# Scores of both components in one two-bank PSUM tile: a two-layer hybrid encoder on one core

## The chip, the core and the metric

The kernel runs on one core of a Trainium2 chip. The core has a matmul engine (TensorE, PE in the profile; its weight loads are listed apart as PEld), a vector engine (DVE), a scalar engine for activations (ACT), a general engine (POOL) and queues that start transfers (SP). PE writes its products into PSUM. Each engine works through its own list of instructions in order and waits on semaphores for the others. The metric is the device time of one execution in microseconds (us); less is better. PSUM is used here as eight banks of 128 partitions by 512 float32 numbers.

## What is computed

A trunk of two encoder layers over 512 tokens of width 1024, in float32:

```python
for l in range(DEPTH):                          # DEPTH = 2
    h = rmsnorm(x, g_attn[l])
    proj = jnp.einsum('bsd,dc->bsc', h, w_in[l])
    qa, ka, va, qb, kb, vb = jnp.split(proj, offs, axis=-1)
    # group A: 8 query heads, 2 kv heads of 64, blocks of 128, keys of +-1 block, a sink per head
    ya = windowed_gqa_sink(qa, ka, va, sink[l])         # after QK-norm and rotary
    # group B: 4 heads, each with two components of 64; softmax of each; values of 128
    #   w = p[:, :, 0] - lam * p[:, :, 1]
    yb = rmsnorm(diff_attention(qb, kb, vb, lam), subln[l]) * (1.0 - lambda_init)
    y = jnp.concatenate([ya, yb], axis=-1)
    x = x + jnp.einsum('bsm,md->bsd', y, w_out[l])
    h = rmsnorm(x, g_ffn[l])
    gate, val = jnp.split(jnp.einsum('bsd,df->bsf', h, w_up[l]), 2, axis=-1)
    gate = centred_dwconv(gate, conv_w[l], conv_b[l])   # width 3 over the tokens
    x = x + jnp.einsum('bsf,fd->bsd', jax.nn.silu(gate) * val, w_down[l])
```

d_ff is 2816, 22 blocks of 128.

## The kernel before

**Products.** Every float32 operand is split into a high and a low part, and a product is three matmuls (high by high, low by high, high by low; the helper `mm3`, L193 to L196). Activations lie transposed: features on partitions, the 512 tokens along the row. Weights come as units of 512 KB or less; ACT makes the high part (L181), DVE or POOL the low one (L182).

**A layer.** The first norm is folded into the input projection (`project`), which runs over nine chunks of 256 columns by four token tiles: akv (keys and values of group A), aq0 and aq1 (its queries), and bv, bq, bk of the two halves of group B. Then attention, the output projection, a second norm, and the feed-forward part (FFN) in two parts of 12 and 10 blocks: for each block gate and value (`up`), the convolution and the gate on DVE, ACT and POOL, and after each part the down projection `dn` into eight output tiles, which DVE adds to the residual (L716).

**Group A**, for each of 2 head pairs `ip` and 4 query blocks `qb`: `a_scores` makes scores for 2 query heads i by 2 kv heads g. The product for g reads the 64 rows of its own half of the array (rows 0 to 63 or 64 to 127), so two neighbours with different g use different halves. DVE adds the mask and takes the maximum (L416), ACT the exponential (L434), DVE normalises (L441). `a_values` transposes the weights on PE, one bank per key block (`pt_a`, L457), splits them (L246, L247) and multiplies by the values (`pv_a`).

**Group B**, for each half, query block and head: `b_scores` makes the scores of both components c, again on the two halves of the array (L502); a maximum for each (L505), an exponential for each (L509), and their difference. `b_values` transposes (`wt_b`, L529) and multiplies by the values (`yb`).

**Banks.** `mm`: two banks, for the projections and the output projection while attention runs. `at`: four single banks, for akv, part of aq, all scores and the transposed weights. `acc`: one for sums over key blocks. `tq`: one, for the transposes of queries, keys and results. In the FFN, for `dn` and for the last pass of the output projection (`out_last(1)`), `wide` (L109) rotates at, at, mm. A tile of a tag waits until the oldest tile of that tag has been read for the last time.

**Order.** `weave` (L665) writes two tracks into each other by cost: attention, and a chain of bv, bq, bk of the two halves and of the output projection. The framework's scheduler then puts each engine's instructions in order by its own times, with the waits that tiles and tags demand.

## Time and profile before

| | |
|---|---|
| median of 3 runs | 1309.32 us (1308.12 to 1310.32) |
| span of the profiled execution, first to last instruction | 1302.4 us |
| time of that execution outside the span | not shown; the median is 6.9 us above its span |
| mean granted TensorE clock | 0.991 |
| busy: PE, PEld, DVE, ACT, POOL | 1270.6, 1056.6, 772.9, 557.5, 385.4 us |
| data moved by the transfers | 102.96 MB, 79 GB/s on the mean |

The profile is of one execution. A row of a group names the line, the engine, the operation, output and inputs with their shapes, the count, then busy us in total, mean ns of one, and the engine's idle time just before with what ended it. A row of the timeline has start and duration in us; matmuls are pipelined, so the distance of two starts, not the duration, is what one costs. A row of windows has the stretch, its length, and for each engine the busy us and the number of instructions, then the granted clock as a share of full speed, the transfers' share and GB/s. The attention of layer 0 lies at about 30 to 290 us, its FFN behind that up to about 650; layer 1 follows in the same way.

### The profile page before, as it was taken

The numbers are of one execution on the slowest core, as the hardware profiler recorded it, in microseconds if no ns is written. First come the engines' busy times: TensorE is split into PE (matmuls) and PEld (weight loads), VectorE is DVE, ScalarE is ACT, GpSimd is POOL, SyncE is SP. The second block draws the span as 40 slices with busy tenths as digits, with TensorE's granted clock in tenths as the row PEclk, the third lists the DMA queues.
The fourth block names the chain that finished last, engine by engine and source line by source line (L and its number), as shares of the span: only waits on it lengthen the run. The fifth ranks groups of instructions, "written<-read, shape, count | busy, mean of one in ns | idle before, by whom it ended". The sixth has DMA issues, their size and how long they took to land. (4 is left out here: it accounts for less than half of the span.)

```text
span 1302.4 us, 17571 instructions
## 1 busy us (share of the span) xinstructions
PE 1270.6 (98%) x6744; PEld 1056.6 (81%) x6744; DVE 772.9 (59%) x1425; ACT 557.5 (43%) x1027; POOL 385.4 (30%) x446
## 2 busy tenths in 40 slices
PE   6999899999999999999999999999899999999998
PEld 6988788687888888888899878877788888888887
DVE  7678787767655324554466786767765543355532
ACT  4566555435433223333455656544443332233321
POOL 6847376114211000110156654741411110011100
PEclk8999999999999999999999999999999999999999
DMA  5211112113332233332331211111133322433232
GB/s 181 91 33 49 58 33 65 33 33 97 98 97 85 85 106 97 98 97 79 100 98 66 65 33 33 56 59 33 33 113 97 97 81 94 117 98 98 79 106 90
DMA packets 32628, 102.96 MB, mean 79 GB/s; under 512 B 3616, under 2 KB 4000, under 8 KB 32544
## 3 DMA queue, kind: packets, MB, share of 16 engines
q1 hardware_dynamic: 32544, 101.84, 25.6%
q8 instruction: 53, 0.87, 0.3%
q14 instruction: 31, 0.25, 0.1%
HBM read 99.73 MB, written 2.10 MB: 78 GB/s over the span
## 5 line engine op out<-in xcount | busy, mean ns | idle before, releaser
L181 ACT CAST wh<-wr 128x1024 fp32r<-128x1024 f32 (+3 forms) x210 | 197.7, 944 | 400.1 <-PE up L195 192.0
L195 PE MATMUL up<-nf_l,wh 128*128 128x512 f32 x704 | 275.3, 391 | 2.3 <-DVE nf_l L213 1.9
L196 PE MATMUL up<-nf_h,wl 128*128 128x512 f32 x704 | 274.5, 390 | 1.2 <-DVE wl L182 0.9
L194 PE MATMUL up<-nf_h,wh 128*128 128x512 f32 x704 | 272.9, 390 | 0.0
L182 DVE TENSOR_TENSOR wl<-wr,wh 128x1024 fp32r<-128x1024 f32 (+3 forms) x174 | 193.3, 1114 | 112.2 <-ACT wh L181 111.8
L702 POOL TENSOR_TENSOR cv<-cv,rb 128x512 f32<-128x512 f32 x44 | 57.8, 1316 | 521.5 <-ACT cv L701 521.5
L195 PEld LDWEIGHTS up<-nf_l,wh 128*128 128x128 f32 x704 | 132.1, 188 | 33.6 <-DVE nf_l L213 6.6
L196 PEld LDWEIGHTS up<-nf_h,wl 128*128 128x128 f32 x704 | 132.1, 188 | 29.7 <-DVE wl L182 2.9
L194 PEld LDWEIGHTS up<-nf_h,wh 128*128 128x128 f32 x704 | 132.2, 188 | 27.6
L195 PE MATMUL dn<-act,wh 128*128 128x512 f32 x352 | 138.5, 394 | 0.0
L196 PE MATMUL dn<-act,wl 128*128 128x512 f32 x352 | 138.4, 394 | 0.0
L194 PE MATMUL dn<-act,wh 128*128 128x512 f32 x352 | 137.9, 393 | 0.0
L182 POOL TENSOR_TENSOR wl<-wr,wh 128x1024 fp32r<-128x1024 f32 x36 | 87.1, 2421 | 89.4 <-ACT wh L181 89.4
L695 DVE TENSOR_TENSOR gp<-up,rb 128x512 f32<-128x512 f32 x44 | 30.3, 693 | 103.4 <-PE up L196 101.8
L703 DVE TENSOR_TENSOR cv<-cv,up 128x512 f32<-128x512 f32 x44 | 30.2, 687 | 82.6 <-POOL cv L702 73.0
L194 PEld LDWEIGHTS dn<-act,wh 128*128 128x128 f32 x352 | 66.0, 188 | 16.0
L195 PEld LDWEIGHTS dn<-act,wh 128*128 128x128 f32 x352 | 66.0, 187 | 15.7
L196 PEld LDWEIGHTS dn<-act,wl 128*128 128x128 f32 x352 | 66.0, 188 | 15.4
L716 DVE TENSOR_TENSOR x<-x,dn 128x512 f32<-128x512 f32 x32 | 22.0, 689 | 78.4 <-PE dn L196 78.4
L509 ACT ACTIVATE e_b<-sc_b,mx_b,rqb 128x512 f32<-128x512 f32 x64 | 49.2, 774 | 38.6 <-DVE mx_b L506 38.6
L701 ACT ACTIVATE cv<-cv 128x512 f32<-128x512 f32 x44 | 27.8, 632 | 76.4 <-DVE cv L700 76.3
L505 DVE TENSOR_REDUCE mx_b<-sc_b 128x1 f32<-128x512 f32 x64 | 42.0, 681 | 0.2
(211 smaller groups left out, 2713.7 us busy)
## 6 DMA issues: line engine op xcount, KB each, us to landing
wr<-w_up SPq DMA_DIRECT2D x88, 512.0 KB, 3.6
wr<-w_in SPq DMA_DIRECT2D x36, 512.0 KB, 3.7
wr<-w_down SPq DMA_DIRECT2D x32, 384.0 KB, 3.1
wr<-w_down SPq DMA_DIRECT2D x32, 320.0 KB, 2.9
wr<-w_out SPq DMA_DIRECT2D x16, 512.0 KB, 3.6
x<-xT SPq DMA_DIRECT2D x8, 256.0 KB, 5.3
outT<-x SPq DMA_DIRECT2D x8, 256.0 KB, 2.0
rows<-row_par SPq DMA_DIRECT2D x2, 260.0 KB, 5.0
```

Of the source, the lines that this page charges most:

```text
L181: nc.scalar.copy(hi[:, o], raw[:, o])
L182: eng.tensor_tensor(out=lo[:, o], in0=raw[:, o], in1=hi[:, o], op=ALU.subtract)
L194: nc.tensor.matmul(acc, lhsT=a[0], rhs=b[0], start=start, stop=False)
L195: nc.tensor.matmul(acc, lhsT=a[0], rhs=b[1], start=False, stop=False)
L196: nc.tensor.matmul(acc, lhsT=a[1], rhs=b[0], start=False, stop=stop)
L505: nc.vector.tensor_reduce(out=mx[:, c:c + 1], in_=sc[c], axis=AX, op=ALU.max)
L509: nc.scalar.activation(e[c], sc[c], AF.Exp, bias=mx[:, c:c + 1], scale=rq[:, c:c + 1], accum_out=lsum[:, 2 * j + c:2 * j + c + 1])
L695: nc.vector.tensor_tensor(out=g[:, 1:S + 1], in0=acc[0], in1=rb, op=ALU.mult)
L701: nc.scalar.activation(cv, cv, AF.Silu)
L702: nc.gpsimd.tensor_tensor(out=cv, in0=cv, in1=rb, op=ALU.mult)
L703: nc.vector.tensor_tensor(out=cv, in0=cv, in1=acc[1], op=ALU.mult)
L716: nc.vector.tensor_tensor(out=x_sb[d], in0=x_sb[d], in1=acc, op=ALU.add)
```

## The change

The four single banks `at` become two tiles of two banks each (`at2`). `both` hands out the two banks of such a tile; `halves` hands them out one after the other; `wide2` hands out pairs, every third one of two `mm` banks. The scores of one query head for both kv heads share a tile, and so do both components of a step of group B, whose two maxima become one reduction of a [128, 2, 512] tile to [128, 2]. Gate and value of a block share a pair. The akv projection, the four middle tiles of aq, `out_last(1)` and `dn` take halves in turn. In `a_values` the transposes go to the first bank of an `at2` tile for key block 0 (the second stays unused), to `tq` for key block 1 and to `mm` for key block 2; in `b_values` `wt` goes to the first bank of an `at2` tile, or as before to `mm` for the second head of the second half. No arithmetic changes.

```diff
@@ -95,8 +95,8 @@
     def mm(name):
         return ps.tile([P, S], F32, tag="mm", bufs=2, name=name)
 
-    def at(name):
-        return ps.tile([P, S], F32, tag="at", bufs=4, name=name)
+    def at2(name):
+        return ps.tile([P, 2, S], F32, tag="at", bufs=2, name=name)
 
     def accum(name):
         return ps.tile([P, S], F32, tag="acc", bufs=1, name=name)
...
@@ -106,9 +106,25 @@
 
     cyc = {"i": 0}
 
-    def wide(name):
+    def wide2(name):
         cyc["i"] += 1
-        return (mm, at, at)[cyc["i"] % 3](name)
+        if cyc["i"] % 3 == 0:
+            return mm(f"{name}a"), mm(f"{name}b")
+        t = at2(name)
+        return t[:, 0], t[:, 1]
+    def halves(pick):
+        have = []
+        def alloc(name):
+            if not have:
+                have.extend(pick(name))
+            return have.pop(0)
+        return alloc
+    def both(name):
+        t = at2(name)
+        return t[:, 0], t[:, 1]
 
     def run(gen):
         for _ in gen:
...
@@ -375,7 +391,7 @@
             split_out(va[0][:, t * P:(t + 1) * P], va[1][:, t * P:(t + 1) * P], raw[:, P:])
             qk_out(raw[:, :P], t, P, tabs[1], ka, "ka", None)
 
-        run(project("akv", akv_done, at))
+        run(project("akv", akv_done, halves(both)))
         rqa = sb.tile([P, NT, 4, 2], F32, tag="rqa", bufs=1, name=f"rqa{l}")
         rqb = sb.tile([P, NT, 4, 2], F32, tag="rqb", bufs=1, name=f"rqb{l}")
         qa = [(pair(f"qah{l}_{i}"), pair(f"qal{l}_{i}")) for i in range(2)]
...
@@ -385,7 +401,8 @@
                 bank, t, CW, tabs[0], qa[i], f"qa{i}", rqa[:, t, 2 * i:2 * i + 2, :].rearrange("p a b -> p (a b)")), alloc)
 
         qk = {}
-        banks = iter((mm, mm, at, at, at, at, mm, mm))
+        pairs_at = halves(both)
+        banks = iter((mm, mm, pairs_at, pairs_at, pairs_at, pairs_at, mm, mm))
         run(proj_a(0, lambda name: next(banks)(name)))
         run(proj_a(1, lambda name: next(banks)(name)))
 
...
@@ -405,7 +422,7 @@
             mx = small(f"mx_{nm}", 4)
             so = []
             for i in range(2):
-                sc = [at(f"sc_{nm}_{i}_{g}") for g in range(2)]
+                sc = both(f"sc_{nm}_{i}")
                 for j, (u, v) in enumerate(((0, 0), (0, 1), (1, 0))):
                     for g in range(2):
                         rs = slice(g * HD, (g + 1) * HD)
...
@@ -450,7 +467,7 @@
             pv = accum(f"pv_{nm}")
             pb = []
             for b in range(nkb):
-                tr = at(f"pt_{nm}_{b}")
+                tr = mm(f"pt_{nm}_{b}") if b == 2 else both(f"pt_{nm}_{b}")[0] if b == 0 else tq(f"pt_{nm}_{b}")
                 for g in range(2):
                     for i in range(2):
                         o = (2 * g + i) * P
...
@@ -495,14 +512,14 @@
             rq = rqb[:, qb, h, :]
             q, k = qk[half]
             e = []
-            sc = [at(f"sc_{nm}_{c}") for c in range(2)]
+            sc2 = at2(f"sc_{nm}")
+            sc = (sc2[:, 0], sc2[:, 1])
             for i, (u, v) in enumerate(((0, 0), (0, 1), (1, 0))):
                 for c in range(2):
                     rs = slice(c * HD, (c + 1) * HD)
                     nc.tensor.matmul(sc[c], lhsT=q[u][rs, j, qb * P:(qb + 1) * P], rhs=k[v][rs, j, :],
                                      start=i == 0, stop=i == 2)
-            for c in range(2):
-                nc.vector.tensor_reduce(out=mx[:, c:c + 1], in_=sc[c], axis=AX, op=ALU.max)
+            nc.vector.tensor_reduce(out=mx, in_=sc2, axis=AX, op=ALU.max)
             nc.vector.scalar_tensor_tensor(out=mx, in0=mx, scalar=-1.0, in1=rq, op0=ALU.mult, op1=ALU.mult)
             for c in range(2):
                 e.append(tmp(f"e_{nm}_{c}"))
...
@@ -524,7 +541,7 @@
                 b_st[half, qb, "acc"] = accum(f"yb{l}_{half}_{qb}")
             yb = b_st[half, qb, "acc"]
             w = b_st.pop((half, qb, j))
-            tr = (mm if half and j else at)(f"wt_{nm}")
+            tr = mm(f"wt_{nm}") if half and j else both(f"wt_{nm}")[0]
             for b in range(NT):
                 nc.tensor.transpose(tr[:, b * P:(b + 1) * P], w[:, b * P:(b + 1) * P], ident)
             wh, wl = prob(f"wth_{nm}"), prob(f"wtl_{nm}")
...
@@ -664,7 +681,7 @@
 
         weave((attend(), ATT),
               (chain(proj_b(0), proj_b(1), out_pass(0, mm), out_pass(1, mm), out_tail()), 98.6))
-        run(out_last(1, w_last, wide))
+        run(out_last(1, w_last, halves(wide2)))
         norm.square(NK - 2)
         norm.square(NK - 1)
         r_tok2 = norm.rms()
...
@@ -675,20 +692,18 @@
         rb = tmp(f"rb{l}")
         nc.scalar.copy(rb, rps)
 
         h = norm
         if l + 1 < depth:
             norm = Norm(l + 1, 0, f"na{l + 1}")
         for pi, (f0, f1) in enumerate(FF_PARTS):
             act = []
             for f in range(f0, f1):
-                acc = []
+                acc = wide2(f"up{l}_{f}")
                 for j in range(2):
                     w = next_unit()
-                    a = wide(f"up{l}_{f}_{j}")
                     for k in range(NK):
-                        mm3(a, (w[0][:, k, :], w[1][:, k, :]), (h.hi[k], h.lo[k]), k == 0, k == NK - 1)
-                    acc.append(a)
+                        mm3(acc[j], (w[0][:, k, :], w[1][:, k, :]), (h.hi[k], h.lo[k]), k == 0, k == NK - 1)
                 g = tmp(f"gp{l}_{f}", S + 2)
                 nc.gpsimd.memset(g[:, 0:1], 0.0)
                 nc.gpsimd.memset(g[:, S + 1:S + 2], 0.0)
...
@@ -705,6 +720,7 @@
                 split_out(a[:, 0], a[:, 1], cv)
                 act.append((a[:, 0], a[:, 1]))
             last = pi == len(FF_PARTS) - 1
+            wide = halves(wide2)
             for d in range(NK):
                 acc = wide(f"dn{l}_{pi}_{d}")
                 nk = f1 - f0
```

What this does to the order of PE's instructions is shown at three places. Lines of the changed kernel lie some 16 to 18 further down; a number behind a tile's name counts buffers, `[waits X]` names the engine whose signal the instruction waits for, x2 is a count of alike neighbours.

**Scores of group B** (layer 0, second half; `sc_b0_2_1_1` is head 2, query block 1, component 1; `wt` are the transposes of an earlier step, `yb` the products with the values). Before:

```order
L541 MATMUL yb0_0_3_2808<-vb0_0_0_850,wtl_b0_1_3_2890 128x128 [waits DVE_49]
L541 MATMUL yb0_0_3_2808<-vb0_0_0_850,wtl_b0_1_3_2890 128x128
L541 MATMUL yb0_0_3_2808<-vb0_0_2_993,wtl_b0_1_3_2890 128x128 x2
L502 MATMUL sc_b0_2_1_1_2926<-bkh0_1_1785,bqh0_1_1783 128x512 [waits PE_49]
L502 MATMUL sc_b0_2_1_1_2926<-bkl0_1_1786,bqh0_1_1783 128x512
L502 MATMUL sc_b0_2_1_1_2926<-bkh0_1_1785,bql0_1_1784 128x512
L529 MATMUL wt_b0_2_0_2960<-ident_72,e_b0_2_0_0_2793 128x128 [waits Activation_49]
L529 MATMUL wt_b0_2_0_2960<-ident_72,e_b0_2_0_0_2793 128x128 x3
L502 MATMUL sc_b0_3_1_0_3001<-bkh0_1_1785,bqh0_1_1783 128x512 [waits Activation_49]
L502 MATMUL sc_b0_3_1_0_3001<-bkl0_1_1786,bqh0_1_1783 128x512
L502 MATMUL sc_b0_3_1_0_3001<-bkh0_1_1785,bql0_1_1784 128x512
L538 MATMUL yb0_1_0_2959<-vb0_1_0_1830,wth_b0_2_0_2965 128x128 [waits Activation_49]
```

The change, at the first scores of head 3:

```order
L558 MATMUL yb0_0_3_2770<-vb0_0_0_844,wtl_b0_0_3_2777 128x128 [waits DVE_49]
L558 MATMUL yb0_0_3_2770<-vb0_0_0_844,wtl_b0_0_3_2777 128x128
L558 MATMUL yb0_0_3_2770<-vb0_0_2_985,wtl_b0_0_3_2777 128x128 x2
L520 MATMUL sc_b0_3_0_2818<-bkh0_1_1767,bqh0_1_1765 128x512 [waits PE_49]
L520 MATMUL sc_b0_3_0_2818<-bkh0_1_1767,bqh0_1_1765 128x512
L520 MATMUL sc_b0_3_0_2818<-bkl0_1_1768,bqh0_1_1765 128x512 x2
L520 MATMUL sc_b0_3_0_2818<-bkh0_1_1767,bql0_1_1766 128x512 x2
L583 MATMUL tr_yb0_0_2_2806<-ident_72,y_yb0_0_2_2734 128x128 [waits DVE_49]
L583 MATMUL tr_yb0_0_2_2806<-ident_72,y_yb0_0_2_2734 128x128
```

The three products of one component stood apart from the other component's three; now the two components' products are neighbours in pairs, on one tile, whose name has no component any more.

**Windowed group, second head pair of layer 0** (`sc_a0_1_2` are the scores of query block 2, `pt` the transposes, `pv` the products with the values, `pj0_bk0`, `pj0_bv1` the projections of the other track, `tr_bk` the transposes of new keys). Before:

```order
L412 MATMUL sc_a0_1_2_0_0_1668<-ka0_213,qah0_1_417 128x384 [waits DVE_49]
L412 MATMUL sc_a0_1_2_0_0_1668<-ka0_213,qah0_1_417 128x384
L412 MATMUL sc_a0_1_2_0_0_1668<-ka0_213,qal0_1_418 128x384
L194 MATMUL pj0_bk0_3_1680<-wh10_808,na0_h0_119 128x256 [waits Activation_49]
L195 MATMUL pj0_bk0_3_1680<-wl10_809,na0_h0_119 128x256
L196 MATMUL pj0_bk0_3_1680<-wh10_808,na0_l0_120 128x256
L194 MATMUL pj0_bk0_3_1680<-wh10_808,na0_h1_123 128x256
L195 MATMUL pj0_bk0_3_1680<-wl10_809,na0_h1_123 128x256
L196 MATMUL pj0_bk0_3_1680<-wh10_808,na0_l1_124 128x256
```

The change, for the same scores:

```order
L474 MATMUL pt_a0_1_0_1_1588<-ident_72,so_a0_1_0_1_1_1386 128x128
L429 MATMUL sc_a0_1_2_1_1676<-ka0_213,qah0_1_415 128x384 [waits DVE_49]
L429 MATMUL sc_a0_1_2_1_1676<-ka0_213,qah0_1_415 128x384 x3
L429 MATMUL sc_a0_1_2_1_1676<-ka0_213,qal0_1_416 128x384 x2
L210 MATMUL pv_a0_1_0_1578<-ph_a0_1_0_1_1593,va0_214 128x512 [waits Activation_49]
L211 MATMUL pv_a0_1_0_1578<-pl_a0_1_0_1_1594,va0_214 128x512 [waits DVE_49]
L212 MATMUL pv_a0_1_0_1578<-ph_a0_1_0_1_1593,va0_214 128x512
L373 MATMUL tr_bk00_2_1642<-ident_72,raw_bk00_2_1628 128x128 [waits PE_49,Pool_49]
L373 MATMUL tr_bk00_2_1642<-ident_72,raw_bk00_2_1628 128x128
L474 MATMUL pt_a0_1_1_0_1707<-ident_72,so_a0_1_1_0_0_1500 128x128 [waits DVE_49]
L474 MATMUL pt_a0_1_1_2_1756<-ident_72,so_a0_1_1_0_0_1500 128x128
L210 MATMUL pj0_bv1_0_1781<-wh12_1096,na0_h0_119 128x256
```

Between the scores of query block 2 stood a run of the projection's matmuls, 17 before the next score; now only scores, values and transposes follow each other, each with its own wait, until the projection `bv1` goes on behind the transposes of key block 2 (`pt_a0_1_1_2`), which are in a bank of `mm`.

**Down projection** (`dn0_0_0` is output tile 0 of the first part of layer 0; in the changed kernel outputs 0 and 1 share the tile that is named after the first, and wh52 is the weight unit of output 1, wh54 that of output 2). Before:

```order
L194 MATMUL dn0_0_0_4567<-act0_11_4564,wh51_4492 128x512 [waits Activation_49]
L195 MATMUL dn0_0_0_4567<-act0_11_4564,wh51_4492 128x512 [waits DVE_49]
L196 MATMUL dn0_0_0_4567<-act0_11_4564,wl51_4493 128x512
L194 MATMUL dn0_0_1_4617<-act0_0_3728,wh52_4523 128x512
L195 MATMUL dn0_0_1_4617<-act0_0_3728,wh52_4523 128x512
L196 MATMUL dn0_0_1_4617<-act0_0_3728,wl52_4524 128x512
```

The change:

```order
L210 MATMUL dn0_0_0_4504<-act0_11_4501,wh51_4431 128x512 [waits Activation_49]
L211 MATMUL dn0_0_0_4504<-act0_11_4501,wh51_4431 128x512 [waits DVE_49]
L212 MATMUL dn0_0_0_4504<-act0_11_4501,wl51_4432 128x512
L210 MATMUL dn0_0_2a_4603<-act0_0_3672,wh54_4530 128x512 [waits Activation_49]
L211 MATMUL dn0_0_2a_4603<-act0_0_3672,wh54_4530 128x512
L210 MATMUL dn0_0_0_4504<-act0_0_3672,wh52_4461 128x512 [waits DVE_49]
L211 MATMUL dn0_0_0_4504<-act0_0_3672,wh52_4461 128x512
L212 MATMUL dn0_0_0_4504<-act0_0_3672,wl52_4462 128x512
```

Output 1 followed output 0 with no wait. Now two matmuls of output 2, which lies in a bank of `mm`, come first, and then output 1 waits for DVE.

## What I predicted, and how

> **What bounds the kernel now.** I read the page's head first, then the chain of waits, then single stages.
>
> ```profile
> span 1302.4 us, 17571 instructions
> ...
> PE 1270.6 (98%) x6744; PEld 1056.6 (81%) x6744; DVE 772.9 (59%) x1425; ACT 557.5 (43%) x1027; POOL 385.4 (30%) x446
> ...
> PE   6999899999999999999999999999899999999998
> DVE  7678787767655324554466786767765543355532
> PEclk8999999999999999999999999999999999999999
> ...
> PE 27%; DVE 0%; issue 0%
> ```
>
> TensorE (PE) is busy for 1270.6 of 1302.4 us, nearly every slice shows 9, and the chain names only PE. So a us taken from PE's own work is a us of the span, and so is a us in which PE waits: it has 32 us of idle time in all, and no slack elsewhere. All other engines have room on average. The average hides the attention stages, where DVE is the second limit:
>
> ```profile
> 70.00:80.00 10.00, 10.00 (x63) 7.90 (x62) 8.05 (x20) 6.59 (x16) 3.92 (x4) 1.00 0.06 6
> 110.00:120.00 10.00, 10.00 (x65) 8.17 (x64) 7.86 (x24) 5.93 (x19) 6.01 (x8) 1.00 0.01 2
> 120.00:130.00 10.00, 10.00 (x72) 8.72 (x71) 9.41 (x22) 7.31 (x19) 8.36 (x9) 1.00 0.18 53
> ```
>
> The columns are the stretch, its length, and the busy us of PE, PEld, DVE, ACT and POOL. PE is full while DVE is busy 8 to 9 us of 10: the projection's matmuls fill every wait of the attention chain. Before is kept full by that filler, and what moves it moves the time.
>
> The sum is made against the profiled execution: 1302.4 us of span. The median of the runs is 1309.3, so 6.9 us lie around the span; I take them as unchanged.
>
> **Gain: score matmuls that pair.** A score matmul uses 64 of the 128 rows; component 0 the one half, component 1 the other. Before gives each its own bank, so each waits for its own release and PE's order mostly runs three for one component, something else, then three for the other. Both cases stand in the trace, in the timeline of PE (start, duration, operation, count):
>
> ```profile
> 268.68 0.49 PE L502 MATMUL sc_b<-bkh,bqh 64*128 64x512 f32 x1
> 269.01 0.39 PE L502 MATMUL sc_b<-bkl,bqh 64*128 64x512 f32 x1
> 269.24 0.39 PE L502 MATMUL sc_b<-bkh,bql 64*128 64x512 f32 x1
> 269.57 0.66 PE L529 MATMUL wt_b<-ident,e_b 128*128 128x128 f32 x4
> 270.06 0.38 PE L566 MATMUL tr_yb<-ident,y_yb 128*128 128x128 f32 x2
> ...
> 882.65 0.50 PE L502 MATMUL sc_b<-bkh,bqh 64*128 64x512 f32 x2
> 882.99 0.40 PE L502 MATMUL sc_b<-bkl,bqh 64*128 64x512 f32 x2
> 883.21 0.40 PE L502 MATMUL sc_b<-bkh,bql 64*128 64x512 f32 x2
> 883.54 0.50 PE L194 MATMUL wo<-yh,wh 128*128 128x512 f32 x1
> ```
>
> Three alone take 269.57 - 268.68 = 0.89 us; six as three pairs take 883.54 - 882.65 = 0.89 us. The second of a pair is free. A step is about 0.226 us (269.01 to 269.24, 882.99 to 883.21), so entering and leaving this mode costs 0.89 - 3 x 0.226 = 0.21 us. In the order of PE, counted over both layers, matmuls that stand alone fall from 148 to 8 for the 512-wide scores, 74 to 8 for the 384-wide and 46 to 6 for the 256-wide: 70, 33 and 20 new pairs. By columns a 384-wide one is worth 0.17 us and a 256-wide 0.115, so 70 x 0.226 + 33 x 0.17 + 20 x 0.115 = 23.7 us. The groups of score matmuls fall from 114 to 75: 39 x 0.21 = 8.2. **Gain 32 us**, bounds 24 (no gain from fewer groups) and 32.
>
> **The fused maximum.** It is one reduction of 1024 columns for two of 512:
>
> ```profile
> L509 ACT ACTIVATE e_b<-sc_b,mx_b,rqb 128x512 f32<-128x512 f32 x64 | 49.2, 774 | 38.6 <-DVE mx_b L506 38.6
> ...
> L505 DVE TENSOR_REDUCE mx_b<-sc_b 128x1 f32<-128x512 f32 x64 | 42.0, 681 | 0.2
> ```
>
> 64 x 0.681 = 43.6 us become 32 x something between 0.681 and 1.36, so DVE gets between 0 and 21.8 us back; near the upper price, since no row here has a cost that is mostly fixed, some 4. The exponential needs both maxima anyway and DVE is not the bound in the second half of attention: 0 on the span.
>
> **Loss 1: a tile is one thing to the scheduler.** The order shows that waits go by tile, not by bank: the second half of a tile is written only after the reader of the first half is done. In the down projection (dn) output d sits in one half and d+1 in the other, and each d is read by the residual add L716. Before rotates whole banks and has no such wait. In its place:
>
> ```profile
> 1298.04 0.39 PE L195 MATMUL dn<-act,wh 128*128 128x512 f32 x1
> 1298.27 0.40 PE L196 MATMUL dn<-act,wl 128*128 128x512 f32 x1
> 1298.71 0.69 DVE L716 TENSOR_TENSOR x<-x,dn 128x512 f32<-128x512 f32 x1 [6.29 <-PE dn L196]
> ```
>
> Steps are 0.23 us; the add begins 0.44 after the last matmul's start, so 0.21 after its slot, and takes 0.69, and with 0.05 for the hop back the next half starts 0.95 us late. The new order puts two matmuls of another output (2 x 0.23) ahead of the wait in eight such places and nothing in three: 8 x 0.5 + 3 x 0.95 = **7 us**. The other halves handed out one by one (akv, aq, out_last) have 6 to 25 matmuls ahead of the same wait, 1.4 us or more: 0. If the scheduler's cover were gone there too, each of these some 14 would cost up to 0.95, 13 us.
>
> The Trainium skill, "PSUM — Partial Sum Buffer", section "PSUM bank collisions raise a hardware error", asks for guards by bank and quadrant only, and two halves of this tile are two banks. By it the wait isn't needed and this term would be 0, the sum 7 us lower. The wait is in the program's order all the same, so the row's price stands.
>
> **Loss 2: the filler of the windowed group.** The third key block's transposes now take a bank of mm, in which the projections run, and the second's the single bank tq. A projection gets its bank behind them, so two stretches per layer lose the filler. In the stretch shown (scores of steps 1 and 2 of the second head pair) DVE has 34 instructions between the maximum of step 1 and the normalised row that the transposes wait for. Their prices:
>
> ```profile
> L247 DVE TENSOR_TENSOR pl_a<-pt_a,ph_a 128x512 fp32r<-128x512 f32 x15 | 10.1, 684 | 1.0 <-ACT ph_a L246 1.0
> L441 DVE TENSOR_SCALAR so_a<-so_a,rl_a 128x384 f32<-128x384 f32 x16 | 9.7, 666 | 0.0
> L416 DVE CUSTOM_DVE_ANT_0 so_a<-sc_a,mask_sb 128x384 f32<-128x384 f32 x16 | 8.7, 546 | 0.1
> L441 DVE TENSOR_SCALAR so_a<-so_a,rl_a 128x256 f32<-128x256 f32 x12 | 6.7, 622 | 0.0
> L247 DVE TENSOR_TENSOR yl<-pv_a,yh 64x256 fp32r<-64x256 f32 x12 | 5.0, 419 | 0.2
> L342 DVE TENSOR_TENSOR raw_bk<-raw_bk,rs_bk 128x256 f32<-128x256 f32 x4 | 4.4, 1104 | 1.9 <-POOL rs_bk L243 1.9
> ...
> L434 ACT ACTIVATE so_a<-so_a,ng_a,rqa 128x384 f32<-128x384 f32 x16 | 11.1, 696 | 0.0
> ...
> L434 ACT ACTIVATION_READ_ACCUMULATOR so_a<-so_a,ng_a,rqa 128x1 f32 x28 | 5.3, 188 | 0.0
> ```
>
> 6 x 0.546 (masked maxima) + 4 x 0.622 + 3 x 0.666 (normalising) + 2 x 0.684 + 5 x 0.42 (low parts) + 1.1 + some 2.6 for 13 small ones = 14.9 us. What PE has beside it:
>
> ```profile
> 703.74 0.63 PE L412 MATMUL sc_a<-ka,qah 64*128 64x384 f32 x4
> 704.21 0.34 PE L412 MATMUL sc_a<-ka,qal 64*128 64x384 f32 x2
> 704.48 0.38 PE L194 MATMUL pj_bv<-wh,na_h 128*128 128x256 f32 x1
> ```
>
> Three groups of six scores at 704.48 - 703.74 = 0.74 us, 32 projection matmuls at 0.12 (below, 21.23 - 21.11), nine of 512 columns at 0.23 and 16 transposes at (270.06 - 269.57) / 4 = 0.12: 10.1 us. So it waits **5 us**, at least 0 (DVE ahead) and at most 10 (DVE late at the start). The earlier stretch, before the first bq projection, is a chain through tq and then behind four exponentials, 4 x (0.696 + 0.188) = 3.5 us, plus the normalising; 10 us if nothing covers it, 0 if all; I take **5**, since the first product's six score matmuls and its own transposes lie beside half of it. Per layer 10, both layers **20 us**, bounds 0 and 40.
>
> **Loss 3: second half of attention.** The transposes of the weights (wt) take a whole two-bank tile, and such a tile comes free only after the second exponential instead of the first: 0.774 + 0.19 later, 0.97 us a step. With 16 steps a layer in which it can decide, bounds are 0 and 15.5 us; the output projection's matmuls stand between most steps, so I take a quarter, 4 a layer, **8 us**.
>
> **Loss 4: ramps.** While the first norm is made, before has four token tiles in flight and after two:
>
> ```profile
> 0.00:23.94 23.94, 13.56 (x73) 12.04 (x73) 0.00 (x0) 0.93 0.62 213
> 23.94:30.20 6.26, 4.49 (x23) 4.22 (x23) 0.47 (x1) 0.75 0.29 86
> ...
> 18.86 0.41 PE L194 MATMUL pj_akv<-wh,na_h 128*128 128x256 f32 x1
> 19.08 0.41 PE L195 MATMUL pj_akv<-wl,na_h 128*128 128x256 f32 x1
> ...
> 21.11 0.28 PE L194 MATMUL pj_akv<-wh,na_h 128*128 128x256 f32 x1
> 21.23 0.28 PE L195 MATMUL pj_akv<-wl,na_h 128*128 128x256 f32 x1
> ```
>
> These rows are of the akv projection alone: 73 of 96 matmuls are done when the last normed slice lands. In the new order 46 stand ahead of that point, so 27 move behind it, at 0.12 (21.23 - 21.11) to 0.21 us (19.08 - 18.86, where the clock was lower): 3.2 to 5.7, I take **4.5**; layer 1 has other work there, 0. At the first FFN step gate and value of one tile no longer interleave with the next: 44 matmuls ahead of the last slice instead of 57 in layer 0, 13 x 0.226 = **3 us**. Three of four up parts now end on a tile whose release is late: **2 us** (0 to 5).
>
> **Sum.** -32 + 7 + 20 + 8 + 4.5 + 3 + 2 = +12.5 on the span: 1314.9 us, and 1309.3 + 12.5 = **1322 us** for the median.
>
> **Rivals.** (R1) *The stalls hide, the pairs win.* When PE stalls, the other engines run ahead, and the next wait finds its operand ready; the stall terms 2 and 3 then go to 0: -32 + 16.5 = -15.5, 1294 us. For it: ACT and POOL are at 4 to 8 of 10 in the rows above. Against: DVE at 8 to 9 of 10 can't run ahead. It decides as soon as losses 2 and 3 together are under 15.5 us. (R2) *A draw:* they sum to 15.5 instead of 28, the time is 1309. (R3) *Stalls cost clock as well.* The trace has matmuls of 256 columns at 0.21 instead of 0.12 us for about 3 us after early idle time (rows at 18.86). If each of six longer stalls brought that, each would cost 3 x (1 - 0.12 / 0.21) = 1.3 us, together 8, and with the stretches of loss 2 at 10 and 8 us (+16) the sum is +36: 1345. Against: its waits are mostly a few us long, with matmuls between. The Trainium skill, "TensorE: Matmul & The Clock Gate", Part 1, has the clock halve after an idle window of about 3.4 us; by it only a single stall of that length counts, which is the 5 us ones here; the trace's 0.21 rows agree with it. (R4) *The pairs are in the order but not in time:* component 1's matmuls wait for an operand or weights of their own, half of the gain (16) stays out, +28.5: 1338. Against: 882.65 shows that pairs run when both are next to each other.
>
> **Chances.** Forecast (1315 to 1330) 0.40, R3 0.14, R4 0.12, R2 (within 1303 to 1315) 0.14, R1 0.20. The likeliest one's own range is 1314 to 1331. The 8-in-10 range takes in R1 and the centre of R3: 1293 to 1346. A measurement of this kernel tells 0.2%, 2.6 us, from no change. Of R2 0.06 lie within that, 0.03 below, 0.05 above: faster 0.23, same 0.06, slower 0.71.
>
> **What would show it.** Gain: PE's busy time down by some 30 us, and score groups of x2 rows everywhere. Loss 1: L716's lines (now at another line) as releaser of PE waits in dn, about 0.5 us eleven times. Loss 2: windows between 60 and 140 us with PE under 9 of 10 and waits for normalised rows. Loss 4: akv ending some 4 us later. It would be wrong if PE's idle time grew by less than 15 us, or if PE's busy time did not fall.

## The result and the profile after

The changed kernel takes 1352.6 us (1350.6 to 1355.6), the kernel before 1309.8: a ratio of 1.033 (95% interval 1.031 to 1.035), 43 us slower. I had forecast 12.5 us slower, with a range up to 1346; the time lies above it.

The head of the page after, its table of slices and its chain:

```profile
span 1349.2 us, 17525 instructions
...
PE 1262.3 (94%) x6744; PEld 1051.1 (78%) x6744; DVE 767.7 (57%) x1393; ACT 555.2 (41%) x1027; POOL 381.9 (28%) x446
...
PE   6989799898999999999999879999899999999998
...
PEclk9989799899999999999999889999999999999999
...
PE 25%; issue 1%; ACT 0%; DVE 0%; POOLq 0%; POOL 0%; ACTq 0%
```

PE's idle time is 1349.2 - 1262.3 = 86.9 us, before 31.8: 55.1 more. Its busy time fell by 8.3 us only, though the pairs are there, and the mean granted clock fell from 0.991 to 0.977. The span grew by 55.1 - 8.3 = 46.8 us. The profiled execution took 1351.0 us with a span of 1349.2, so 1.8 us lie outside the span and not the 6.9 that I had carried over; every later execution of the kernel before has 1.7 to 1.9 (1311.1 us beside a span of 1309.3). The profiled execution before was thus some 5 us faster than the median of its runs, and that is why the spans differ by 46.8 us and the medians by 43. The table of PE's waits after says for what (us in total, times, longest):

```profile
PE pt_a L474 <- DVE so_a L458: 24.0, 6, 5.8
...
PE tr_qa L373 <- DVE qal L263: 3.6, 4, 1.0
PE yb L558 <- DVE wtl_b L263: 3.4, 6, 0.9
...
PE dn L210 <- DVE x L732: 1.7, 2, 0.9
```

The first is the wait of loss 2: transposes of group A's weights for the normalised rows, 1.5 us before and 24.0 now. The windows of layer 0's group A after (busy us of PE, PEld, DVE, ACT, POOL, then the granted clock):

```profile
80.00:90.00 10.00, 5.22 (x24) 2.95 (x23) 3.77 (x13) 5.45 (x16) 3.60 (x2) 0.76 0.36 107
90.00:100.00 10.00, 8.46 (x54) 7.92 (x55) 6.72 (x25) 5.57 (x15) 0.00 (x0) 0.73 0.00 0
130.00:140.00 10.00, 4.43 (x27) 2.91 (x24) 6.72 (x17) 5.97 (x16) 9.47 (x9) 0.82 0.16 53
140.00:150.00 10.00, 7.70 (x30) 4.74 (x30) 5.78 (x18) 4.47 (x12) 3.27 (x5) 0.67 0.19 52
```

The two stretches that the prediction named are there, PE half empty, and behind the empty time the clock is at 0.67 to 0.82 where it was 1.00. DVE is no longer at 8 to 9 of 10 but at 4 to 7: it too now stands still for part of the time. The timeline of PE shows what the clock does:

```profile
91.50 0.90 PE L474 MATMUL pt_a<-ident,so_a 128*128 128x128 f32 x3 [3.23 <-DVE so_a L458]
...
92.84 0.41 PE L210 MATMUL pj_bq<-wh,na_h 128*128 128x256 f32 x1
93.06 0.41 PE L211 MATMUL pj_bq<-wl,na_h 128*128 128x256 f32 x1
...
140.26 1.43 PE L474 MATMUL pt_a<-ident,so_a 128*128 128x128 f32 x4 [5.83 <-DVE so_a L458]
...
152.47 0.44 PE L474 MATMUL pt_a<-ident,so_a 128*128 128x128 f32 x2 [3.32 <-DVE so_a L458]
```

Behind the stall of 3.23 us a step of 256 columns is 0.22 us (93.06 - 92.84) instead of 0.12. By the first matmul of each stage in the timelines of both kernels, the 46.8 us divide as follows, beside what the prediction's terms come to for the same stage:

| stage | measured | predicted |
|---|---|---|
| layer 0 to the first score of group A | +7.0 | +4.5 |
| to the first score of group B | +17.1 | +4.2 |
| to the first up matmul | -7.1 | -6.2 |
| FFN, to the first akv of layer 1 | +10.2 | +7.5 |
| layer 1 to the first score of group A | +1.5 | 0 |
| to the first score of group B | +17.8 | +4.2 |
| to the last score of group B | -4.6 | -6.2 |
| to the last dn | +4.9 | +4.5 |

The rows are stretches between two marks in PE's order, and work that moves across a mark moves from one row to another.

Predicted for group A is 10 of stalls less 5.8 of gain, for group B 4 less 10.2. Group A is 26.5 of the 34.3 us that are missing.

### The profile page after: what moved, and what is told of

Its sections match the earlier page's. It is cut to its first block, busy times and chain, and to the rows that moved or that the text cites. A ratio compares the mean times of both kernels' runs of the same rounds, so it can differ in the third digit from the quotient of the medians.

```text
span 1349.2 us, 17525 instructions
## 1 busy us (share of the span) xinstructions
PE 1262.3 (94%) x6744; PEld 1051.1 (78%) x6744; DVE 767.7 (57%) x1393; ACT 555.2 (41%) x1027; POOL 381.9 (28%) x446
## 5 line engine op out<-in xcount | busy, mean ns | idle before, releaser
L211 PE MATMUL up<-nf_l,wh 128*128 128x512 f32 x464 | 181.1, 390 | 3.6 <-DVE nf_l L229 3.6
L212 PE MATMUL up<-nf_h,wl 128*128 128x512 f32 x464 | 180.7, 390 | 0.1
L210 PE MATMUL up<-nf_h,wh 128*128 128x512 f32 x464 | 180.8, 390 | 0.0
L211 PEld LDWEIGHTS up<-nf_l,wh 128*128 128x128 f32 x464 | 87.1, 188 | 23.7 <-DVE nf_l L229 5.8
L210 PE MATMUL dn<-act,wh 128*128 128x512 f32 x240 | 95.7, 399 | 6.4 <-ACT wh L197 3.4
L210 PEld LDWEIGHTS up<-nf_h,wh 128*128 128x128 f32 x464 | 87.1, 188 | 18.3 <-ACT nf_h L228 0.3
L212 PEld LDWEIGHTS up<-nf_h,wl 128*128 128x128 f32 x464 | 87.0, 188 | 18.3 <-DVE wl L198 0.6
L211 PE MATMUL dn<-act,wh 128*128 128x512 f32 x240 | 95.5, 398 | 0.4 <-DVE act L263 0.4
L212 PE MATMUL dn<-act,wl 128*128 128x512 f32 x240 | 94.4, 396 | 0.0
L210 PEld LDWEIGHTS dn<-act,wh 128*128 128x128 f32 x240 | 45.3, 189 | 20.5 <-ACT wh L197 5.6
L474 PE MATMUL pt_a<-ident,so_a 128*128 128x128 f32 x160 | 29.7, 307 | 27.5 <-DVE so_a L458 24.0
L211 PEld LDWEIGHTS dn<-act,wh 128*128 128x128 f32 x240 | 45.4, 189 | 11.5 <-DVE act L263 1.1
L474 PEld LDWEIGHTS pt_a<-ident,so_a 128*128 128x128 f32 x160 | 20.5, 155 | 33.5 <-DVE so_a L458 27.6
```

The lines of the kernel that those rows point to most:

```text
L210: nc.tensor.matmul(acc, lhsT=a[0], rhs=b[0], start=start, stop=False)
L211: nc.tensor.matmul(acc, lhsT=a[0], rhs=b[1], start=False, stop=False)
L212: nc.tensor.matmul(acc, lhsT=a[1], rhs=b[0], start=False, stop=stop)
L474: nc.tensor.transpose(tr[:, o:o + P], so[2 * i + g][:, b * P:(b + 1) * P], ident)
```

## The experiments

The kernels here are made so that each stage takes either single banks, as before, or the two-bank tiles, as in the change; what isn't named is as before. Ratios are to the kernel before, run beside each of them (1306 to 1308 us). Kernels that mix the two kinds close the four banks and open them anew where a stage begins; what that alone costs was not measured.

### Which stage costs what

```diff
+    def phase(ph):                    # called at the start of each stage
+        want = DOUBLE[ph]             # e.g. {"in": False, "a": False, "b": True, "f": False}
+        if bank["double"] is want: return
+        ...                           # close the pool of the four banks, open it anew
-        return ps.tile([P, S], F32, tag="at", bufs=4, name=name)
+        return bank["pool"].tile([P, S], F32, tag="at", bufs=4, name=name)     # or [P, 2, S], bufs=2
```

> The two-bank tiles in group B alone (scores, fused maximum, wt); the input projection, group A, out_last, up and dn keep the four single banks, and the order of those stages is as before. Theory 1, the stages add: between the first score of group B and the first up matmul the changed kernel took 7 us less than before in layer 0 and about 5 less in layer 1, so this kernel should take 1309.7 - 12 = 1297 us (1294 to 1301), faster than both. Rival: group B gained there only because the stalls of group A had let the other engines and the weights run ahead; then nothing is gained, 1308 to 1312 us.

Measured: 1299.4 us, 0.994 (0.993 to 0.996): theory 1. The tiles in group B alone make the kernel faster.

> The two-bank tiles in the input projection and group A alone; group B and the FFN keep the single banks. Theory 1, the stages add: +7 and +5 us up to the first score of each layer, +17 and +18 us from there to the first score of group B, so 1309.7 + 47 = 1357 us (1350 to 1362), with waits of PE for normalised rows (so_a) of some 24 us. Rival: part of group A's loss comes from the two-bank scores of group B that begin while group A ends; then 1335 to 1348 us.

Measured: 1349.4 us, 1.033 (1.030 to 1.037), with 25.1 us of waits for so_a: just under theory 1's range and above the rival's. Group A with the input projection costs as much as the whole change.

> The two-bank tiles in out_last, up and dn alone; attention and the input projection as before. Theory 1: the waits by tile in dn (7 us), the later first step (3) and the tails of up (2) cost what the prediction took, 1309.7 + 12 = 1322 us (1317 to 1326). Rival: these waits are hidden because the two matmuls ahead and the weights' casts cover them, 1309 to 1313 us.

Measured: 1326.6 us, 1.015 (1.012 to 1.018), a little over theory 1.

> The two-bank tiles in the input projection alone (akv and part of aq). If the ramp sets the start of group A, 7 and 5 us are lost: ratio to before 1.006 to 1.011. Rival, from the run without it, which was only 1 us faster than with it: group A takes up a late start, ratio 0.999 to 1.003.

Measured: 1312.9 us, 1.005 (1.003 to 1.007): between the two.

> The two-bank tiles in group A alone; the input projection, group B and the FFN keep single banks. If the stages add, the ramp's 12 us go and group A's loss of 17 a layer stays: 1306.9 + 42.5 - 12 = 1337 us, ratio 1.021 to 1.027. Rival: group A loses because it starts late against the projections that run beside it; with the ramp repaired most of it goes, ratio under 1.015.

Measured: 1348.2 us, 1.032 (1.029 to 1.034). The rival falls, and the simple sum too: the late start costs 6.7 us by itself, and beside group A's stalls 1 to 2 us, which is within the intervals. The stages don't add to the change either: group A and the projection 42.5, FFN 19.7, group B -7.5 make 54.7 instead of 43. One candidate is the clock at a place that was not changed. Here are the windows of the FFN's run, of the kernel before, and of the run with short stalls shown further down, which has single banks everywhere, all three in the attention of layer 0, where nearly all of their order is the same:

```profile
230.00:245.00 15.00, 14.38 (x55) 11.02 (x54) 7.76 (x19) 5.36 (x13) 0.78 (x2) 0.66 0.12 37
```

```profile
230.00:245.00 15.00, 14.38 (x80) 10.88 (x79) 10.25 (x25) 7.68 (x19) 0.70 (x2) 1.00 0.13 37
```

```profile
230.00:245.00 15.00, 14.38 (x55) 10.97 (x55) 7.78 (x19) 5.50 (x13) 0.93 (x2) 0.66 0.13 37
```

PE is busy for 14.38 of 15 us in all three, with a clock of 0.66, 1.00 and 0.66: (1.00 - 0.66) x 15 = 5 us of full clock. The third has no two-bank tile at all, so the FFN's tiles are not needed for this loss. Whether it is part of the 12 us between 54.7 and 43 is not shown.

### Why group A stalls

One line sets where the transposes of group A's weights go; single banks everywhere:

```diff
-                tr = at(f"pt_{nm}_{b}")
+                tr = at(...) if b == 0 else tq(...) if b == 1 else mm(...)     # a_route
+                tr = (mm if b == 2 else at)(f"pt_{nm}_{b}")                     # r_mm
+                tr = (tq if b == 1 else at)(f"pt_{nm}_{b}")                     # r_tq
```

> Single banks everywhere, as before; only the transposes of group A's weights are routed as in the change: key block 0 in at, 1 in tq, 2 in mm. Theory 1, the routing takes the projection's filler away: 10 us and more a layer, ratio to before 1.012 to 1.025. Theory 2, the routing does no harm while scores and transposes share four tiles; two tiles of two banks are too few for group A: ratio 0.997 to 1.005, and hardly any wait of PE for normalised rows (so_a; 25.1 us with the two-bank tiles in group A).

Measured: 1354.1 us, 1.036 (1.034 to 1.039): theory 1, and more than it. With single banks, and without a tile of two banks anywhere, the routing alone costs as much as the change. Its waits:

```profile
PE pt_a L496 <- DVE so_a L480: 17.5, 6, 4.5
...
PE tr_qa L394 <- DVE qal L284: 4.3, 3, 2.2
PE tr_bk L394 <- DVE bkl L284: 3.2, 1, 3.2
```

> Single banks everywhere; of the change's routing only one part: the transposes of key block 2 of group A go to mm, in which the projections run, the others stay in at. Theory 1, projections queue behind transposes in mm and PE has no filler: most of the routing's loss is here, ratio to before 1.018 to 1.034, with PE waiting over 10 us for normalised rows (so_a). Theory 2, the loss comes from the single bank tq, where transposes of weights, queries and keys wait for each other: ratio under 1.010.

> Single banks everywhere; only the transposes of key block 1 go to tq, the others stay in at. Theory 1 (mm is the cause): ratio to before 0.998 to 1.010. Theory 2 (tq is the cause): 1.018 to 1.034.

Measured: mm 1320.6 us, 1.011 (1.009 to 1.014); tq 1339.7 us, 1.026 (1.024 to 1.029). Both count, tq most: 1.026 lies in theory 2's range, and mm's 1.011 just above the 1.010 that theory 2 allowed. The two together, 1.037, make up the 1.036 of the whole routing. The prediction had told the story mainly by mm.

Then the other way, in the changed kernel: all transposes in halves of the two-bank tiles, or only those of key block 1 taken from tq into a tile:

```diff
-                tr = mm(...) if b == 2 else both(...)[0] if b == 0 else tq(...)
+                tr = pt2(f"pt_{nm}_{b}")            # pt_halves: pt2 = halves(both), anew for each step
+                tr = mm(...) if b == 2 else both(...)[0]                        # tqfree
```

> The changed kernel, but all transposes of group A's weights take halves of the two-bank tiles, none a bank of mm or tq. Theory 1, the filler: the stalls of group A come from projections that queue behind transposes in mm and from the single tq; with both free, group A loses some 12 us a layer less, 1352.6 - 24 = 1329 us (1322 to 1338). Rival: two tiles for scores and transposes of group A are too few whatever is done with mm; then the stalls move and the time stays within 1346 to 1360 us.

> The changed kernel, but the transposes of key block 1 of group A take the first bank of a two-bank tile like those of key block 0, instead of tq. Theory: tq is the larger half of the routing's loss in the change too (with single banks 1.026 for tq against 1.011 for mm), so some 25 us go: ratio to before 1.010 to 1.020. Rival: the two tiles of two banks are then what group A waits for, as in the run with all transposes in halves of them: 1.028 to 1.050.

Measured: 1366.6 us, 1.046 (1.043 to 1.050), and 1359.0 us, 1.039 (1.037 to 1.042). Both theories fail. The second rival holds; the first was right that the stalls move, but the time went past its 1360 us: taken back into the two tiles, the transposes cost more than in tq and mm. So either is enough for the loss: the routing with four single banks (1.036), or two tiles for scores and transposes with less of the routing (1.039) or none (1.046). In the run with halves some of the waits are different ones, for the operation that makes the weights' low part (`pl_a`): the products with the values wait for its result, the next transposes for it to have read their tile:

```profile
PE pt_a L497 <- DVE so_a L480: 10.6, 10, 2.5
PE pv_a L232 <- DVE pl_a L284: 6.5, 4, 1.8
...
PE pt_a L497 <- DVE pl_a L284: 5.2, 3, 2.4
```

### What a stall costs beside its length

```diff
+                if b == 0 and (ip, qb) in WARM:        # {(0, 1): 12, (1, 1): 18, (1, 2): 12}
+                    tr2 = mm(f"pt_{nm}_2")             # overwritten by the transposes later
+                    for _ in range(WARM[ip, qb]):
+                        nc.tensor.matmul(tr2, lhsT=va[0][:, :P], rhs=va[0], start=True, stop=True)
```

> The changed kernel with 42 more matmuls of 512 columns in each layer, on values that nobody reads, ahead of the transposes of three steps of group A at which PE stood still longest. They do no useful work (84 x 0.226 = 19 us of PE time if nothing hides them). Theory: a third to a half of group A's loss is the lower clock after these stalls (the clock lost 32 us of the span here and 12 before); busy through the stalls PE keeps its clock, and the time falls to 1330 to 1345 us. Rival: the stalls alone count and the clock recovers beside them; then the time stays at 1350 us or rises by up to 19 us.

Measured: 1361.8 us, 1.043 (1.041 to 1.046), mean clock 0.976. The stalls moved to other instructions (5.6 us at a transpose of new keys, 4.4 at a bq projection), the clock was as low as without, and 9 to 13 of the added 19 us were paid (by the times and by the ratios). The time lies in the rival's range, but as the stalls only moved, this run settles nothing on the clock. So I measured its price by itself, in the FFN, where PE before stands still for 1.8 us a layer only:

```diff
+                if f in (3, 7, 15, 19):
+                    nc.scalar.activation(zst[:, 0:1], acc[1][:, 0:1], AF.Copy, scale=0.0)
+                    for _ in range(LONG):                        # 2 or 12
+                        nc.gpsimd.tensor_tensor(out=zst, in0=zst, in1=zst, op=ALU.mult)
+                    ...                # PE transposes zst; later products are queued behind it
```

> The kernel before with 8 short stalls of PE in its up stages (four a layer, each at the end of a block): a transpose that nobody reads waits for ACT and two POOL operations that start from that block's last product, and all later products are queued behind it. Nothing else changes. Theory: a stall shorter than about 3 us costs its own length and no clock: the time grows by PE's added idle time, and the time lost by the lower clock stays at 10 to 18 us over the span. Rival: any stall lowers the clock; the span grows by 1.5 us a stall more than the idle time.

> The same 8 stalls with twelve POOL operations each instead of two, some 6 us. Theory: stalls of this length are followed by matmuls at half the clock, and each costs 1.5 to 3.4 us on top of its idle time; the span grows by 12 to 27 us more than the idle time. Rival: the span grows by the idle time alone, and the clock that was lost in the changed kernel was no cost of its own.

Measured: 1344.7 us, 1.028 (1.025 to 1.032), and 1390.1 us, 1.062 (1.059 to 1.066). The waits in the one and the other:

```profile
PE zt L759 <- POOL zst L757: 23.6, 8, 2.9
```

```profile
PE zt L759 <- POOL zst L757: 66.0, 8, 8.3
```

From the first up matmul to the next stage's first matmul (in layer 1 to the last dn) the FFN takes 367.7 and 367.4 us before, 385.6 and 385.2 with the short stalls, 409.6 and 410.0 with the long ones. That is 35.7 us for 23.6 of idle time, and 84.5 for 66.0: **a stall of 2.9 us costs 1.5 us beside its length, one of 8.3 us costs 2.3**. Some of that is not clock: two of the short stalls were followed by no slow steps and cost 0.35 us each beside their length, for the added transpose and for starting again; the other six cost 1.7 to 2.0. The rest of each run's growth lies outside the FFN, 5 us of it in the window at 230 to 245 us shown above. My theory that a stall under some 3 us is free falls; that the long ones cost 1.5 to 3.4 holds. The timeline behind a long stall:

```profile
356.96 0.48 PE L759 MATMUL zt<-ident,zst 128*128 128x128 f32 x1 [8.25 <-POOL zst L757]
...
358.09 0.63 PE L243 MATMUL up<-nf_h,wl 128*128 128x512 f32 x1
358.52 0.63 PE L241 MATMUL up<-nf_h,wh 128*128 128x512 f32 x1
...
360.64 0.39 PE L243 MATMUL up<-nf_h,wl 128*128 128x512 f32 x1
360.87 0.39 PE L241 MATMUL up<-nf_h,wh 128*128 128x512 f32 x1
```

Steps of 0.43 us instead of 0.23 for some 3.5 us here, 2.7 to 4.8 in all cases. Behind the short stalls such a stretch came in six of eight cases, in four of them not at once but a few steps later. The Trainium skill, "TensorE: Matmul & The Clock Gate", Part 1, puts the idle window that halves the clock, and the busy one that restores it, at about 3.4 us each. The length of the slow stretches fits the second; the idle time of 2.9 us that was enough here is somewhat less than the first.

### The waits within a tile

```diff
+                for i in mms[d]:
+                    if d: tc.declare_no_dep(i.ins, adds[d - 1].ins, reason="other bank")
...
+                for i in ups[1]: tc.declare_no_dep(gp.ins, i.ins, reason="other bank")
```

> The two-bank tiles in out_last, up and dn alone, and the waits between the two banks of one tile are taken out for dn (an output's matmuls no longer wait for the add of the output before, which reads the other bank) and for up (gate's first multiply no longer waits for value's matmuls). The banks differ, so nothing that a bank holds is touched. Theory 1, the loss in the FFN is these waits and the weights' casts that come late behind them: ratio to before 1.003 to 1.008 in place of 1.015, with the first step's 4 us left. Rival: it is the pairwise release of banks, whatever the waits: 1.012 to 1.016.

Measured: 1311.7 us, 1.002 (1.000 to 1.004), where the same tiles with the waits had 1.015: theory 1, and a little better than its range. These waits between the two banks of one tile are 13 of the FFN's 15 thousandths. The FFN itself says the same: with the tiles it takes 378.9 and 374.9 us, without these waits 372.6 and 366.8, before 367.7 and 367.4, so 14.4 of 18.7 us go. No wait of dn for the add or for the weights' high part is left among PE's waits. The first step's waits stay in both runs:

```profile
PE up L233 <- DVE nf_l L252: 3.6, 5, 0.7
```

All five lie in layer 0; before had 1.9 us in 2 waits, one in each layer.

### Pairs without the tile

```diff
-                    for g in range(2):
+                    for g in (1, 0):
                         ...
-                        nc.tensor.matmul(sc[g][:, :n], ...)
+                        mi = nc.tensor.matmul(sc[g][:, :n], ...)
+                        if prev is not None:
+                            tc.add_manual_dep(mi.ins, prev.ins.name, ...)     # issue order only
+                        prev = mi
```

> The kernel with two-bank tiles in group B alone, and in group A single banks, but the six score matmuls of a query head are kept in one order with the heads alternating, so that they mostly stand side by side (77 pairs instead of 36). Theory: pairs are free, so PE saves some 41 x 0.15 = 6 us more: ratio to before 0.988 to 0.992. Rival: the fixed order makes PE wait for the second bank, and the gain is lost: 0.994 to 1.000.

Measured: 1285.7 us, 0.983 (0.981 to 0.986). Faster than both kernels, by 22 us against before and 67 against the change, and more than either theory said. Its page:

```profile
span 1285.5 us, 17549 instructions
...
PE 1245.9 (97%) x6744; PEld 1042.1 (81%) x6744; DVE 771.1 (60%) x1393; ACT 554.6 (43%) x1027; POOL 386.7 (30%) x446
```

PE's busy time is 24.7 us less than before with the same 6744 matmuls. Against the run with the tiles in group B alone PE is busy for 4.9 us less (1250.8), which is what the theory's 6 us spoke of, and idle for 6.1 us less (39.6 against 45.7); why the idle time fell is not shown.

## Why the prediction was wrong

**What held.** PE bounds the kernel, and idle time of PE is span. Pairs are free: in the run above PE's busy time falls by 24.7 us, against 24 to 32 predicted. The fused maximum takes 1.215 us for two of 0.681, 32 x 0.147 = 4.7 us of DVE (4 predicted). Group B came out at -7.1 and -4.6 us against -6.2 a layer, and PE's idle time from its first score to the first up matmul grew by 3.1 and 5.4 us, 8.5 against the 8 of loss 3; the run with group B alone has the sign. Loss 1 was right in kind and nearly in size, with 9.5 us of PE's waits in dn over both layers against 7 (the FFN's stage is at +10.2 and +4.9 against 7.5 and 4.5); but most waits in dn are put down to the weights' high part, not to the add as I had said:

```profile
457.98 0.50 PE L211 MATMUL dn<-act,wh 128*128 128x512 f32 x1 [0.17 <-DVE act L263]
...
459.44 0.50 PE L210 MATMUL dn_2a<-act,wh 128*128 128x512 f32 x1 [0.73 <-ACT wh L197]
...
680.45 0.47 PE L210 MATMUL dn<-act,wh 128*128 128x512 f32 x1 [0.87 <-DVE x L732]
```

Why the cast comes late I can only argue: output d+1 and d+2 now take weights in another order than they come. Removing the waits by tile removed both kinds. Loss 4 at the first FFN step is five waits of 0.7 and one of 0.8 less the 1.4 of before, 3.0 as predicted; in layer 1 the 1.4 of before are gone, which I had not foreseen:

```profile
313.59 0.50 PE L211 MATMUL up<-nf_l,wh 128*128 128x512 f32 x1 [0.69 <-DVE nf_l L229]
...
322.62 0.50 PE L212 MATMUL up_1a<-nf_h,wl 128*128 128x512 f32 x1 [0.80 <-DVE wl L198]
```

At the first projection loss 4 was 7.0 instead of 4.5, and only 1.4 of it is idle time. The rest is slower steps: after, PE still takes 0.21 us for 256 columns up to 33.9 us, where before it takes 0.12 from 30.6 us on. The profile's clock does not show this, as it stands at 1.00 there:

```profile
31.19 0.41 PE L211 MATMUL pj_aq<-wl,na_h 128*128 128x256 f32 x1
31.40 0.41 PE L212 MATMUL pj_aq<-wh,na_l 128*128 128x256 f32 x1
...
30.00:34.00 4.00, 4.00 (x21) 4.00 (x21) 1.25 (x5) 0.98 (x3) 1.45 (x4) 1.00 0.03 10
```

**What failed is loss 2, "the filler of the windowed group".** The waits came in both places and for the rows that it named, but its size was not right: 20 us predicted for both layers, while group A lost 17.1 and 17.8 net of a gain of 5.8 a layer, 46.5 together. Two steps in it went wrong.

First, the stall itself. In the second stretch I set DVE's 14.9 us against PE's 10.1 and took the difference, 5 us, as if the two ran side by side. The waits there are 5.83 + 0.96 + 3.32 = 10.1 us, the upper bound of 10. DVE was busy only 6 to 7 us of 10 there, so the two did not run side by side; that the chain passes from PE to DVE to ACT and back, through the one bank tq, is my reading of the waits. The first stretch has 0.80 + 1.01 + 0.92 + 0.33 + 3.23 = 6.3 us against 5. The rows of these waits that are not shown above, four of the first stretch and one of the second:

```profile
81.63 0.41 PE L373 MATMUL tr_qa<-ident,raw_qa 128*128 128x128 f32 x2 [0.80 <-DVE qal L263]
83.05 0.41 PE L373 MATMUL tr_qa<-ident,raw_qa 128*128 128x128 f32 x2 [1.01 <-DVE qal L263]
84.39 0.66 PE L474 MATMUL pt_a<-ident,so_a 128*128 128x128 f32 x4 [0.92 <-DVE qal L263]
85.37 1.01 PE L429 MATMUL sc_a<-ka,qah 64*128 64x384 f32 x4 [0.33 <-DVE mx_a L433]
...
143.09 1.01 PE L429 MATMUL sc_a<-ka,qah 64*128 64x384 f32 x4 [0.96 <-DVE pl_a L263]
```

A sum of busy times on one engine is a lower bound of such a chain, and I used it as its value. Over the whole of group A, PE's idle time grew by 17.6 and 15.9 us, 33.5 against the 20 of loss 2.

Second, the clock. I put it in rival R3 at 1.3 us for each of six stalls, gave that 14%, and left it out of the sum. Three stalls of 2.7 to 5.8 us a layer and several of about 1 us brought it into group A: added up over stretches of 1 us, the lower clock takes 7.8 and 8.8 us of PE's busy time there, 1.7 in each layer before. So the 17.1 us of layer 0 are 17.6 of idle time and 6.1 of clock less a gain of 6.6, the 17.8 of layer 1 are 15.9 and 7.1 less 5.2. Over the whole span the mean clock fell from 0.991 to 0.977, which is 11.7 and 31.0 us of full clock; by the same stretches 11.4 of the 19 us between them fall on PE's busy time, the others on time in which it stood still anyway. With some 9 us for the slow opening that the clock does not show (an estimate: 49.4 us of busy time up to the first score, against 43.7 before less 3.3 for its clock) that is why PE's busy time fell by 8.3 us only: 8.3 + 11.4 + 9 = 28.7, within the 24 to 32 of the gain. R3 (1345 us) is the case that came, a little too small. The stalls measured by themselves show that this price is no rival but a term of the sum: 1.5 us and more for each stall of 2.9 us.

R1, that the other engines run ahead during a stall and the stall terms vanish, did not come: the idle time of group A grew by more than its term. R4 did not either: the pairs run as pairs.

**What stays open.** Why routing through tq costs 1.026 and through mm 1.011 is shown as a total, not step by step. Whether group A with two-bank scores and the transposes in single banks of their own would gain can't be built in eight banks beside mm, acc and tq, and wasn't tried. Why the runs of single stages sum to 55 and not to 43 is not explained.

## What to carry to other kernels

Two banks in one tile are one thing to whoever tracks it: share a tile only where both halves are written together and read together, as the two score components of group B are, and get the pairing elsewhere by the order of issue alone. Before moving a small product into a bank that another stream uses, look at what is queued behind that bank; here, with PE 98% busy, that routing alone cost as much as the whole change. And where a change makes the bounding engine wait, add some 1.5 to 2.3 us for each stall of 3 to 8 us, mostly for the clock, from the start and not as a rival.

## What I had not expected of the hardware

A stall of PE of 2.9 us was followed in six of eight cases by some 3.5 us at half the clock. And the price of a score matmul on half of the array's rows depends on its neighbour so plainly: six as three pairs take 0.89 us, three alone take 0.89 us. Over the kernel's 384 score matmuls the pairing came with 25 us less of PE's busy time, gained in the end by a shared tile in group B and by order alone in group A. The third thing is the clock of 0.66 shown above, in a stretch that was as full and nearly the same in order as one with 1.00; it came in the two runs with added stalls in the FFN as well, whose attention has single banks as before. What brought it, no run here shows.
